# A hybrid attention and convolution block: narrow tap rows, even halves of the latents, early last sums and other costs in the list scheduler

## The chip, the cores and the metric

The kernel runs on one core of a Trainium2 chip. Five engines work at once and are kept in step by semaphores: PE (TensorE, matmuls), DVE (VectorE), ACT (ScalarE), POOL (GpSimd) and SP (SyncE, which issues the DMAs here). The metric is the device time of one execution in microseconds, lower is better. It is a median of several runs; the trace comes from one further execution, the profiled one.

## The reference, cut to what matters

One layer of a residual block on 512 tokens of width 1024, all in float32:

```
mod = silu(c) @ W_ada + b_ada        # shift, scale, gate of the mixer, shift, scale, gate of the MLP
h   = rms_norm(x) * (1 + scale1) + shift1
z   = h @ w_in                       # [GLU 2048 | q latent 384 | kv latent 256 | rotary key 64 | gates 2048]
A:  u = ua * sigmoid(ub); u = causal depthwise conv(u, 31 taps); y_a = silu(layer_norm(u)) @ w_conv_out
B:  q, k, v from rms_norm of the latents; causal attention of 8 heads; y_b = o @ w_attn_out
x  += gate1 * rms_norm((sigmoid(g_a) * y_a + sigmoid(g_b) * y_b) @ w_out)
h   = rms_norm(x) * (1 + scale2) + shift2
x  += gate2 * rms_norm(relu(h @ w_mlp_in)^2 @ w_mlp_out)
```

The six parts of `mod`, 1024 numbers each, are needed before anything that uses them: the first two ahead of all of `z`.

## The kernel before, in words

**Three matmuls for one.** Every float32 operand is split into a rounded high part and a low remainder (`split` and class `W`: a CAST on ACT writes the high part, a TENSOR_TENSOR on DVE the low one). A product is high by high, high by low and low by high (`mm3`, three matmuls). So each weight tile costs a DMA, an ACT cast, a DVE subtraction, and then matmuls of 128 rows by up to 512 columns.

**The order.** Nothing is issued while the program is written. `Planner.record` notes each operation with a cost (`Planner.cost`), and `Planner.plan` is a list scheduler: it simulates the engines and one DMA pipe with those costs and lets each engine take, of the operations that are ready, the one with the earliest due time (`dead`, counted back from the PE order) less a bonus (`hurry`). PE takes its operations in program order, apart from a few that are put ahead. From the simulated times the two SBUF arenas (`f_arena` for raw floats, `r_arena` for split parts) and PSUM get their places, and the plan is made again with the buffers that result, `PASSES` times. In the end each engine runs a fixed list, strictly in that order; an instruction that waits holds up all that stands behind it on its engine.

**The stages**, in order:

- The first products. `ada_load` brings the columns of W_ada for a group of 128-column slices k of shift1 and scale1; DVE sums them over the partitions' eight row blocks (`KGRP`, SCALAR_TENSOR_TENSOR with `cT`), PE adds over partitions (four matmuls by `ones`), DVE writes `mod`. Then `first_products(k)` makes h of slice k (two ACT ACTIVATEs with `mod`, one DVE subtraction) and multiplies it with the first seven GLU column blocks (`g1_load`, 128x896 of w_in per k; 21 matmuls per k). The last slices are k = 6 and k = 7.
- The small loads. The bias and gain vectors, the positions and the convolution's taps `conv_w` (31 rows of 1024 floats, one DMA of 31x1024) are loaded on the side. After the first products PE transposes them to columns; the taps take eight transposes of 31x128 each and a DVE copy into `cw`.
- The latents (`lat_gemm`). The 704 columns of q latent, kv latent and rotary key are made as 512 columns (weights in four units of 2x512) and 192 columns (two units of 4x192), 96 matmuls each. `lat_norm` normalizes them: per token tile two Squares with a sum on ACT, two ACT Identities of 128x1 and two POOL powers of 128x1 (`rstd`), two ACT multiplications.
- The rest of the GLU, and the convolution: 248 DVE operations of 128x512 (`conv_ops`), which `pump` and the planner spread over the stages as filler: 31 taps for each of eight channel tiles, 240 of them SCALAR_TENSOR_TENSOR with `cw`.
- Attention of eight heads (`proj`, `scores`, `pv`); DVE applies the mask to four score tiles of each head. Then y_b, the gates, the LayerNorm of the convolution (transposes, a statistic on ACT and DVE, a power, diagonal matrices that PE multiplies by `ones`), y_a, and, on DVE along the way, the rest of W_ada (`ada_units`, 128x1024 SCALAR_TENSOR_TENSOR with `cT`).
- `w_out`, the norm behind it, then the MLP. Its second product goes over the hidden units in chunks with a Strassen-like scheme (`strassen`, `banked`): sums of products are added on DVE into `f_arena`, and in the last chunk each finished 128x512 block gets its square sum on ACT, a power on POOL, and two DVE operations before it is stored.

## Time and profile before

| | us |
|---|---|
| median of 3 runs (833.59 to 836.13) | 834.04 |
| the profiled execution, its own time | 832.68 |
| its span, first to last instruction | 830.9 |
| busy in it: PE | 805.1 (97%) |
| busy: DVE | 686.6 (83%) |
| busy: ACT | 422.4 (51%) |
| busy: POOL | 26.4 (3%) |

The granted TensorE clock was 0.994 over the span. The profile lists almost all instructions under one line (L388 before), since a helper issues them; rows are told apart by operation, tiles and shape. In a timeline row stand the start, the time from start to end of a group of like instructions, engine, operation, tiles, shapes and count, and in square brackets the engine's idle time before it and who ended it. Some matmul records are missing from the trace, so that a count can be a little low.

### The profile page before, as it was taken

What the parts mean: (1) busy time and instruction counts of PE and PEld (TensorE: products, weight loads), DVE (VectorE), ACT (ScalarE), POOL (GpSimd) and SP (SyncE); (2) the same over time, 40 slices, a digit from 0 to 9 for tenths busy, and PEclk for the clock granted to TensorE, in tenths of its full rate; (3) what the DMA queues carried; (4) which work ended last, traced back from release to release, by engine and by line L of the source; (5) the groups of instructions that cost most, each with busy time, mean ns of one, the idle gap of its engine ahead of it and who ended that gap; (6) DMA issues with size and microseconds to landing.
All of it is one profiled execution on the core that took longest, in us unless ns stands there. A gap on an engine that the chain in (4) does not pass through costs nothing.

```text
span 830.9 us, 10647 instructions
## 1 busy us (share of the span) xinstructions
PE 805.1 (97%) x3940; PEld 672.5 (81%) x3940; DVE 686.6 (83%) x1012; ACT 422.4 (51%) x712; POOL 26.4 (3%) x84
## 2 busy tenths in 40 slices
PE   6989999999999999999999989999999999999995
PEld 3867888889987888888877879888888888888884
DVE  4979989999999999998999589298529993975696
ACT  5364273275884356218424387375346354554642
POOL 2001020000000000000000020000000000000001
PEclk9999999999999999999999999999999999999998
DMA  9998423201464140062799362065014831660302
GB/s 309 321 301 261 153 70 95 71 27 44 135 176 116 40 126 26 26 229 76 277 341 374 118 205 79 27 195 160 0 51 149 277 131 52 193 212 1 102 0 103
DMA packets 86824, 117.28 MB, mean 141 GB/s; under 512 B 7275, under 2 KB 60628, under 8 KB 86771
## 3 DMA queue, kind: packets, MB, share of 16 engines
q1 hardware_dynamic: 86770, 116.59, 43.6%
q8 instruction: 31, 0.51, 0.2%
q14 instruction: 23, 0.18, 0.1%
HBM read 108.18 MB, written 8.39 MB: 140 GB/s over the span
## 4 chain that ended last, share of the span: by engine, by line
PE 87%; DVE 6%; DMA 4%; ACT 2%; issue 1%; POOL 0%; POOLq 0%; DVEq 0%; ACTq 0%; SPq 0%
PE psum L388 87%; DVE f_arena L388 4%; DMA f_arena<-in_w_in_dram 2%; DVE r_arena L388 1%; ACT f_arena L388 1%; DMA f_arena<-in_w_out_dram 1%; ACT r_arena L388 1%; POOL stats L388 0%; DMA f_arena<-in_x_dram 0%; DMA f_arena<-in_w_ada_dram 0%; ACT stats L388 0%; POOLq L1630 0%; DVE mod L388 0%; DVEq L1630 0%; DVE cols L388 0%
## 5 line engine op out<-in xcount | busy, mean ns | idle before, releaser
L388 PE MATMUL psum<-r_arena 128*128 128x512 f32 (+3 forms) x3592 | 765.7, 373 | 8.5 <-ACT r_arena L388 3.6
L388 PEld LDWEIGHTS psum<-r_arena 128*128 128x128 f32 x3592 | 631.3, 189 | 126.8 <-ACT r_arena L388 4.9
L388 DVE TENSOR_TENSOR r_arena<-f_arena,r_arena 128x1024 fp32r<-128x1024 f32 (+4 forms) x232 | 248.1, 1093 | 97.2 <-PE psum L388 56.2
L388 ACT CAST r_arena<-f_arena 128x1024 fp32r<-128x1024 f32 (+4 forms) x222 | 209.3, 967 | 189.7 <-PE psum L388 123.5
L388 DVE SCALAR_TENSOR_TENSOR f_arena<-f_arena,cw 128x512 f32<-128x512 f32 x240 | 164.5, 748 | 0.0
L388 ACT ACTIVATE f_arena<-psum 128x512 f32<-128x512 f32 x64 | 38.1, 598 | 131.4 <-PE psum L388 124.6
L388 DVE TENSOR_TENSOR f_arena<-f_arena 128x1024 f32<-128x1024 f32 (+3 forms) x78 | 77.3, 1006 | 5.5 <-ACT f_arena L388 3.6
L388 ACT ACTIVATE f_arena<-f_arena 128x512 f32<-128x512 f32 (+3 forms) x100 | 58.5, 606 | 13.5 <-DVE f_arena L388 12.6
L388 DVE SCALAR_TENSOR_TENSOR f_arena<-f_arena,cT 128x256 f32<-128x256 f32 (+2 forms) x84 | 55.3, 705 | 0.2
L388 PE MATMUL psum<-ident,f_arena 128*128 128x128 f32 (+1 forms) x240 | 34.4, 283 | 7.5 <-DVE f_arena L388 7.5
L388 PEld LDWEIGHTS psum<-ident,f_arena 128*128 128x128 f32 (+1 forms) x240 | 28.9, 146 | 12.8 <-DVE f_arena L388 8.2
L388 DVE TENSOR_TENSOR f_arena<-psum,f_arena 128x512 f32<-128x512 f32 x52 | 35.4, 687 | 4.4 <-PE psum L388 4.3
L388 ACT CAST r_arena<-psum 128x512 fp32r<-128x512 f32 (+2 forms) x57 | 30.3, 567 | 16.6 <-PE psum L388 16.4
L388 DVE TENSOR_TENSOR r_arena<-psum,r_arena 128x512 fp32r<-128x512 f32 (+2 forms) x57 | 35.7, 658 | 2.5 <-ACT r_arena L388 1.9
L388 POOL TENSOR_TENSOR stats<-stats,nhalf 128x1 f32<-128x1 f32 x24 | 16.8, 708 | 485.4 <-ACT stats L388 485.4
L388 ACT COPY f_arena<-psum 128x512 f32<-128x512 f32 (+4 forms) x42 | 19.9, 501 | 22.1 <-PE psum L388 21.9
L388 ACT ACTIVATE r_arena<-f_arena 128x512 fp32r<-128x512 f32 (+3 forms) x20 | 13.0, 648 | 18.7 <-DVE f_arena L388 16.2
L388 DVE CUSTOM_DVE_ANT_0 f_arena<-psum,mask 128x128 f32<-128x128 f32 (+3 forms) x32 | 15.2, 487 | 2.6 <-PE psum L388 2.5
L388 DVE SCALAR_TENSOR_TENSOR f_arena<-f_arena 128x512 f32<-128x512 f32 (+1 forms) x18 | 13.4, 747 | 0.3
L388 DVE SCALAR_TENSOR_TENSOR f_arena<-f_arena,psum 128x512 f32<-128x512 f32 x16 | 11.0, 685 | 3.1 <-PE psum L388 2.6
L388 DVE TENSOR_SCALAR f_arena<-f_arena,stats 128x1024 f32<-128x1024 f32 x8 | 6.0, 752 | 8.4 <-POOL stats L388 8.4
L388 DVE SCALAR_TENSOR_TENSOR f_arena<-psum,stats,f_arena 128x512 f32<-128x512 f32 x8 | 5.6, 748 | 8.5 <-POOL stats L388 8.3
(94 smaller groups left out, 188.0 us busy)
## 6 DMA issues: line engine op xcount, KB each, us to landing
f_arena<-in_w_ada_dram SPq DMA_DIRECT2D x16, 1024.0 KB, 8.2
f_arena<-in_w_mlp_in_dram SPq DMA_DIRECT2D x32, 512.0 KB, 4.3
f_arena<-in_w_mlp_out_dram SPq DMA_DIRECT2D x32, 512.0 KB, 5.2
f_arena<-in_w_in_dram SPq DMA_DIRECT2D x28, 512.0 KB, 4.7
f_arena<-in_x_dram SPq DMA_DIRECT2D x8, 512.0 KB, 8.0
f_arena<-in_w_ada_dram SPq DMA_DIRECT2D x16, 256.0 KB, 5.7
f_arena<-in_w_ada_dram SPq DMA_DIRECT2D x8, 512.0 KB, 6.4
h_spill<-r_arena SPq DMA_DIRECT2D x16, 256.0 KB, 4.1
```

Source lines behind the costliest of these rows:

```text
L388: getattr(self.real[o.eng], o.fn)(*o.a, **o.k)
```

## The change

- The taps are loaded as rows of 128 floats (512 B), 248 of them, in three DMAs of 128, 112 and 8 rows, and transposed in two matmuls (128 and 120 columns) instead of eight.
- `lat_gemm` makes two halves of 352 columns (eight weight units of 2x352) instead of 512 and 192.
- `lat_norm` folds the mean's factor into the Squares and takes one Identity of 128x8 and one power of 128x8 for all eight norms; all multiplications come behind it. While that power is planned, POOL's result counts as 4000 ns late (`SLOW`).
- The sums of the MLP's last chunk get the bonus `HG` (`banked`).
- The planner's costs are others: a DMA issue 375 for 475 ns, a DMA's time by its packets (13 ns and 0.0385 ns per byte of a row, over 16 engines) instead of its bytes, its tail 1100 for 910 ns, twice its own time ahead of its due time; a matmul at least 109 ns and 13.3 ns over its columns, where 64 and 2.5 stood; 213 ns for a float32 matmul of one column. `PASSES` is 14 for 8. Since costs set due times, the order of all engines and the places in the arenas are others.

```
-PASSES = 8
+PASSES = 14
+SLOW = 4000.0
...
         if fn == "dma_start":
-            return 475.0, 2000.0
+            return 375.0, 2000.0
...
             if ins[0].dtype == F32:
-                return max(53.5, n / 2.4 + 2) * 4, 190.0
-            return max(64.0, n / 2.4 + 2.5), 190.0
+                return (213.0 if n == 1 else max(53.5, n / 2.4 + 2) * 4), 190.0
+            return max(109.0, n / 2.4 + 13.3), 190.0
...
+        o.post += self.slack if eng == "pool" else 0.0
...
-            o.dma = b
+            n = min(self.run(outs[0]), self.run(ins[0]), 4096)
+            o.dma = b * (13.0 + 0.0385 * n) / (16 * n)
...
-            lat = o.post + (o.dma / 180.0 if o.dma else 0.0)
+            lat = o.post + (2.0 * o.dma if o.dma else 0.0)
...
-                        dma_free = st + o.dma / 360.0
-                        o.t1 = dma_free + 910.0
+                        dma_free = st + o.dma
+                        o.t1 = dma_free + 1100.0
...
-        cwr = fa.alloc(D)
-        sp.dma_start(out=fa.v(cwr)[:TAPS, :], in_=conv_w)
+
+        cwr = fa.alloc(2 * P)
+        cw_rows = conv_w.rearrange("t (a p) -> (t a) p", p=P)
+        for r0, r1, at in ((0, P, 0), (P, P + 112, 0), (P + 112, TAPS * KD, 112)):
+            c0 = P if r0 else 0
+            sp.dma_start(out=fa.v(cwr)[at:at + r1 - r0, c0:c0 + P], in_=cw_rows[r0:r1])
...
-        for ct in range(KD):
-            pe.transpose(pb.v(bc)[:, 128 + ct * 32:128 + ct * 32 + TAPS], fa.v(cwr)[:TAPS, ct * P:(ct + 1) * P],
-                         ident[:TAPS, :TAPS])
+        for i, n in enumerate((P, TAPS * KD - P)):
+            pe.transpose(pb.v(bc)[:, (1 + i) * P:(1 + i) * P + n], fa.v(cwr)[:n, i * P:(i + 1) * P], ident[:n, :n])
...
         def lat_gemm():
+            NL = (QL + KL + DR) // 2
...
-                w = wunit(w_in, k0, C_QL, 2, 512)
+                w = wunit(w_in, k0, C_QL, 2, NL)
...
-            ws = [wunit(w_in, kh, C_R2, 4, 192) for kh in (0, 4)]
+            ws = [wunit(w_in, kh, C_QL + NL, 2, NL) for kh in range(0, KD, 2)]
...
         def lat_norm():
+            s = stat(4 * NT)
             for t in range(NT):
-                s = stat(4)
...
-                rstd(s[:, 2:3], s[:, 0:1], 1.0 / QL)
-                rstd(s[:, 3:4], s[:, 1:2], 1.0 / KL)
...
+            plan.slack = SLOW
+            rstd(s[:, 2 * NT:], s[:, :2 * NT], 1.0)
+            plan.slack = 0.0
...
             def banked(mi, nh, bs):
+                plan.hurry = HG if ch == NCH - 1 else 0.0
+                add_block(mi, nh, bs)
+                plan.hurry = 0.0
```

What this does to the lists is seen at three places. The first is ACT at the end of the first products. ACTIVATEs with `mod` make h of slices k = 4, 5, 6 and 7 in pairs (one to `r_arena`, one to `f_arena`); CASTs of 128x896 are weights of the first products, of 128x512 those of the later GLU tiles, of 128x1024, 768 and 704 those of the latents. Before:

```order
27 L388 ACTIVATE r_arena<-f_arena,mod 128x512
28 L388 ACTIVATE f_arena<-f_arena,mod 128x512
29 L388 CAST r_arena<-f_arena 128x896
30 L388 CAST r_arena<-f_arena 128x512
31 L388 ACTIVATE r_arena<-f_arena,mod 128x512
32 L388 ACTIVATE f_arena<-f_arena,mod 128x512
33 L388 CAST r_arena<-f_arena 128x512
34 L388 CAST r_arena<-f_arena 128x1024 x3
35 L388 CAST r_arena<-f_arena 128x768
36 L388 CAST r_arena<-f_arena 128x1024
37 L388 ACTIVATE r_arena<-f_arena,mod 128x512
38 L388 ACTIVATE f_arena<-f_arena,mod 128x512
```

and now:

```order
28 L405 ACTIVATE r_arena<-f_arena,mod 128x512
29 L405 ACTIVATE f_arena<-f_arena,mod 128x512
30 L405 CAST r_arena<-f_arena 128x896
31 L405 ACTIVATE r_arena<-f_arena,mod 128x512
32 L405 ACTIVATE f_arena<-f_arena,mod 128x512
33 L405 CAST r_arena<-f_arena 128x896
34 L405 CAST r_arena<-f_arena 128x512
35 L405 CAST r_arena<-f_arena 128x704 x2
36 L405 ACTIVATE r_arena<-f_arena,mod 128x512
37 L405 ACTIVATE f_arena<-f_arena,mod 128x512
```

The cast of a GLU tile no longer stands ahead of the pair of k = 6, and ahead of the pair of k = 7 stand two casts for the latents in place of five.

The second is DVE at the sixth head. ISA rows with `mask` are its four masked score tiles (the ISA rows of 128x1 read their sums), and SCALAR_TENSOR_TENSOR with `cw` is the convolution's filler. Before:

```order
249 L388 SCALAR_TENSOR_TENSOR f_arena<-f_arena,cw 128x512 x3
250 L388 ISA f_arena<-psum,mask 128x128
251 L388 ISA f_arena 128x1
252 L388 ISA f_arena<-psum,mask 128x256
253 L388 ISA f_arena 128x1
254 L388 SCALAR_TENSOR_TENSOR f_arena<-f_arena,cw 128x512
255 L388 ISA f_arena<-psum,mask 128x384
256 L388 ISA f_arena 128x1
257 L388 RECIPROCAL f_arena<-f_arena 128x1 x2
258 L388 SCALAR_TENSOR_TENSOR f_arena<-f_arena,cw 128x512
259 L388 ISA f_arena<-psum,mask 128x512
```

and now:

```order
264 L405 SCALAR_TENSOR_TENSOR f_arena<-f_arena,cw 128x512 x3
265 L405 ISA f_arena<-psum,mask 128x128
266 L405 ISA f_arena 128x1
267 L405 SCALAR_TENSOR_TENSOR f_arena<-f_arena,cw 128x512
268 L405 ISA f_arena<-psum,mask 128x256
269 L405 ISA f_arena 128x1
270 L405 RECIPROCAL f_arena<-f_arena 128x1
271 L405 SCALAR_TENSOR_TENSOR f_arena<-f_arena,cw 128x512
272 L405 ISA f_arena<-psum,mask 128x384
273 L405 ISA f_arena 128x1
274 L405 RECIPROCAL f_arena<-f_arena 128x1
275 L405 SCALAR_TENSOR_TENSOR f_arena<-f_arena,cw 128x512
```

One more filler operation stands among the tiles, and more stand ahead of them: over the whole list, of the 240 filler operations 109 stood ahead of the sixth head's last mask tile before and 124 do now, and 113 ahead of the eighth's, where it is 130 now.

The third is DVE at the start of `w_out`. SCALAR_TENSOR_TENSOR with `psum` are the last of the sixteen that the GLU tiles and `co_evac` make, which `w_out`'s products need; the operations of 128x1024 with `cT` (28 of them SCALAR_TENSOR_TENSOR, 4 TENSOR_SCALAR) are the late sums of W_ada; TENSOR_TENSOR of 128x1024 are low parts of weights. Before:

```order
418 L388 SCALAR_TENSOR_TENSOR f_arena<-f_arena,cT 128x1024
419 L388 SCALAR_TENSOR_TENSOR f_arena<-f_arena,psum 128x512
420 L388 TENSOR_TENSOR r_arena<-f_arena,r_arena 128x512
421 L388 TENSOR_TENSOR f_arena<-f_arena 128x512
422 L388 SCALAR_TENSOR_TENSOR f_arena<-f_arena,psum 128x512
423 L388 TENSOR_SCALAR f_arena<-f_arena,cT 128x1024
424 L388 TENSOR_TENSOR f_arena<-f_arena 128x512
425 L388 SCALAR_TENSOR_TENSOR f_arena<-f_arena,cT 128x1024
426 L388 TENSOR_TENSOR r_arena<-f_arena,r_arena 128x1024
427 L388 SCALAR_TENSOR_TENSOR f_arena<-f_arena,cT 128x1024
428 L388 TENSOR_TENSOR r_arena<-f_arena,r_arena 128x1024
429 L388 SCALAR_TENSOR_TENSOR f_arena<-f_arena,cT 128x1024 x3
```

and now:

```order
436 L405 SCALAR_TENSOR_TENSOR f_arena<-f_arena,psum 128x512
437 L405 TENSOR_TENSOR r_arena<-f_arena,r_arena 128x512
438 L405 TENSOR_TENSOR f_arena<-f_arena 128x512
439 L405 TENSOR_TENSOR r_arena<-f_arena,r_arena 128x1024
440 L405 TENSOR_TENSOR r_arena<-f_arena,r_arena 128x512
441 L405 SCALAR_TENSOR_TENSOR f_arena<-f_arena,cT 128x1024
442 L405 TENSOR_TENSOR r_arena<-f_arena,r_arena 128x1024 x4
443 L405 SCALAR_TENSOR_TENSOR f_arena<-f_arena,psum 128x512 x2
444 L405 TENSOR_TENSOR f_arena<-f_arena 128x512 x2
445 L405 TENSOR_TENSOR r_arena<-f_arena,r_arena 128x1024
446 L405 TENSOR_TENSOR r_arena<-f_arena,r_arena 128x512 x2
447 L405 TENSOR_TENSOR r_arena<-f_arena,r_arena 128x1024 x2
```

Behind the last of the sixteen stood 17 of the 32 late sums before, and 8 do now (those of the MLP's gate, far behind): nine of them have moved ahead of it.

On PE, 31 matmuls stand now between the last transposes of the LayerNorm and its matmuls by `ones`, where 44 stood; and the gate row's four matmuls by `onesr`, which had 24 others between them, now follow each other.

37 lines of the change are left out of this document (26 added, 11 removed).

## The prediction

> **What bounds the kernel now.** I read the chain of waits first, then the busy times by stage (the windows), then the timeline of the stages that stand out. From the chain (start, length, what, count):
>
> ```profile
> 50.23 10.22 DMA f_arena<-in_w_in_dram
> 69.76 178.40 PE psum L388 x1041
> 248.81 163.60 PE psum L388 x745
> 431.07 6.41 DMA f_arena<-in_w_out_dram
> 490.70 328.19 PE psum L388 x1544
> ```
>
> From 69.76 on the chain is PE, broken only around 412 to 447 and 475 to 490. Ahead of 69.76 it goes through DMAs and DVE. The windows (busy time and count of PE, PEld, DVE, ACT, POOL, then the granted clock, the DMA share and GB/s) say how much PE loses where:
>
> ```profile
> 0.00:70.00 70.00, 59.34 (x272) 43.56 (x272) 50.55 (x120) 37.68 (x56) 6.89 (x56) 1.00 0.98 305
> 70.00:250.00 180.00, 179.65 (x1046) 158.43 (x1047) 168.63 (x331) 101.66 (x229) 8.65 (x16) 1.00 0.35 108
> 70.00:434.42 364.42, 364.07 (x1886) 310.54 (x1887) 344.86 (x588) 183.13 (x368) 10.06 (x17) 1.00 0.39 123
> 430.00:450.00 20.00, 17.22 (x71) 13.18 (x70) 16.87 (x19) 8.21 (x10) 0.00 (x0) 0.91 1.04 380
> 475.00:500.00 25.00, 22.32 (x141) 19.33 (x140) 20.87 (x29) 21.22 (x44) 6.31 (x7) 1.00 0.59 204
> ```
>
> PE idles 10.7 us in the first 70, 0.35 in the next 364, 2.8 at 430 to 450 (at a clock of 0.91, so that it loses more there) and 2.7 at 475 to 500. DVE is the second limit: of the 364.42 us it is busy 344.86 and idle only 19.6, 11.4 of them before 250. What can be won is PE work itself, the start, and those two gaps; what can be lost is that DVE comes too late.
>
> **The start.** Timeline rows (idle before and its releaser in brackets):
>
> ```profile
> 41.95 0.24 SPq L388 DMA_DIRECT2D f_arena<-in_conv_w_dram  x1
> 46.96 0.16 DVE L388 TENSOR_TENSOR mod<-psum,cols 128x1 f32<-128x1 f32 x1
> 52.51 0.50 PE L388 MATMUL psum<-ones,f_arena 128*128 128x1 f32 x4
> 52.87 2.35 PE L388 MATMUL psum<-r_arena 128*128 128x512 f32 x9
> 53.08 0.62 ACT L388 CAST r_arena<-f_arena 128x512 fp32r<-128x512 f32 x1 [6.12 <-DMA f_arena<-in_w_in_dram]
> 55.91 0.50 PE L388 MATMUL psum<-r_arena 128*128 128x512 f32 x1 [0.69 <-DVE r_arena L388]
> 56.77 0.15 DVE L388 TENSOR_TENSOR mod<-psum,cols 128x1 f32<-128x1 f32 x1
> 56.91 4.60 PE L388 MATMUL psum<-r_arena 128*128 128x512 f32 x19 [0.50 <-DVE r_arena L388]
> 61.42 0.81 ACT L388 ACTIVATE r_arena<-f_arena,mod 128x512 fp32r<-128x512 f32 x1
> 62.28 0.50 PE L388 MATMUL psum<-r_arena 128*128 128x512 f32 x1 [0.78 <-ACT r_arena L388]
> 63.72 4.87 PE L388 MATMUL psum<-r_arena 128*128 128x512 f32 x20 [0.93 <-DVE r_arena L388]
> ```
>
> `mod` of k = 6 is there at 47, but its ACTIVATEs stand on ACT behind the cast of a GLU tile, which waits 6.12 us for a DMA, to 53.08. `mod` of k = 7 could follow the sums of 52.51, and comes at 56.77, since DVE stands on the late ACTIVATEs of k = 6; its own ACTIVATEs run at 61.42, behind five casts of latent weights. PE gets its last first products at 63.72 and ends them at 68.59. The DMA that held ACT was issued next to `conv_w`; what was issued before and after it (KB, us to landing), and the DMA engines between 44.5 and 50:
>
> ```profile
> f_arena<-in_w_ada_dram SPq DMA_DIRECT2D x3, 256.0 KB, 5.9
> f_arena<-in_w_in_dram SPq DMA_DIRECT2D x2, 256.0 KB, 10.2
> DMA  9999999999999976554232010107696786859999
> ```
>
> Before `conv_w` a transfer lands in 5.9 us, behind it in 10.2, and meanwhile the share of the 16 engines falls to zero: one engine still works on something, 4.3 us long. (The Trainium skill, DMA: Bandwidth & Descriptors, section on why a DMA increments its semaphore by 16, says that a transfer is split over the largest number up to 16 that divides its outermost sizes; that makes one engine of 31 rows, 16 of 128 and of 112 rows, eight of 8. The share of zero agrees.)
>
> After the change 112, 128 and 8 rows lie on many engines, and the lists help apart from that: the casts that waited stand behind the ACTIVATEs of k = 6, and two casts instead of five ahead of those of k = 7. Against it, about 0.87 MB (GLU weights of 256 and 512 KB, and the taps) now stand ahead of the last W_ada loads in SP's queue: at the 305 GB/s of the first row 2.9 us, less the 4.3. So the inputs come no later. If PE runs from 52.87 without a wait, the 50 matmuls recorded there (9, 1, 19, 1 and 20) take 50 x 0.227 = 11.4 us (21.76 us for 96, below) and end at 64.2: **-4.4 us**, from -1.5 (inputs 2.9 us later after all) to -5.2 (of the 10.7 us that PE idles in the first 70, the brackets here hold 2.9; a tenth of the other 7.8 on top).
>
> **PE's own work.** The two parts of the latents, a stretch of 256-column matmuls, and the old tap transposes:
>
> ```profile
> 75.62:97.38 21.76, 21.76 (x98) 18.02 (x96) 20.89 (x33) 7.24 (x10) 0.00 (x0) 1.00 0.65 210
> 97.38:108.08 10.70, 10.70 (x98) 10.70 (x96) 10.69 (x17) 4.66 (x17) 0.00 (x0) 1.00 0.13 38
> 492.24 7.68 PE L388 MATMUL psum<-r_arena 128*128 128x256 f32 x62
> 70.80 0.67 PE L388 MATMUL psum<-ident,f_arena 31*128 31x31 f32 x8
> ```
>
> A matmul of 512 columns takes 227 ns, one of 192 takes 111, one of 256 takes 124. The 192s are dear: PE's weight load is busy all of their 10.70 us. For 352 columns the line from 256 to 512 gives 124 + 96 x 0.402 = 163 ns, columns alone 156, the line from 192 to 512 169. So 192 x 0.163 = 31.3 against 32.46 us; I take the middle of 0 and 2.5: **-1.3**. (The Trainium skill, TensorE: Matmul & The Clock Gate, Part 1, "Wait — 56ns, not 53.3ns?", gives N / 2.4 GHz + about 2.5 ns start to start. By it 96 x (215.8 + 82.5) and 192 x 149.2 are the same 28.6 us, and the halves save nothing. The trace speaks against it for narrow matmuls: 111 ns where it has 82.5.)
>
> Eight transposes become two: **-0.3** of 0.67, either way by 0.2. The single power costs nothing:
>
> ```profile
> L388 POOL TENSOR_TENSOR stats<-stats,nhalf 128x1 f32<-128x1 f32 x24 | 16.8, 708 | 485.4 <-ACT stats L388 485.4
> L388 POOL TENSOR_TENSOR lns<-lns,nhalf 128x4 f32<-128x4 f32 x1 | 1.4, 1402 | 256.2 <-DVE lns L388 256.2
> 129.88 2.78 PE L388 MATMUL psum<-ident,f_arena 128*128 128x128 f32 x24
> ```
>
> Width 8 lies between 0.7 and 2 x 1.4 us, and PE has other work from 108.08 to the latents' transposes at 129.88. Without that cover it would cost up to 2.8.
>
> **DVE's order.** Filler and late sums (start, length, count):
>
> ```profile
> 344.91 8.05 DVE L388 SCALAR_TENSOR_TENSOR f_arena<-f_arena,cw 128x512 f32<-128x512 f32 x12
> 440.95 3.67 DVE L388 SCALAR_TENSOR_TENSOR f_arena<-f_arena,cT 128x1024 f32<-128x1024 f32 x3
> 434.42 0.69 DVE L388 SCALAR_TENSOR_TENSOR f_arena<-f_arena,psum 128x512 f32<-128x512 f32 x1 [0.83 <-PE psum L388]
> 437.29 1.20 PE L388 MATMUL psum<-r_arena 128*128 128x512 f32 x4 [2.44 <-ACT r_arena L388]
> ```
>
> The 17 fillers that now stand ahead of the last head are 17 x 0.67 = 11.4 us, just what DVE idled before 250. The nine late sums that moved ahead of the last `co_evac` are 8 x 1.22 + 0.75 = 10.5 us more DVE work ahead of 434.42. PE will want that operation 6.0 us earlier than before (4.4 + 1.3 + 0.3). DVE without any idle would reach it at 434.42 - 19.6 + 10.5 - 4.4 = 420.9, PE wants it at 428.4: DVE may idle 7.5 us on the way, where it idled 19.6. With the fillers in the holes 19.6 - 11.4 = 8.2 are left: PE waits **+0.7**, between 0 and 12.1 if no hole is filled.
>
> For it, the sums no longer hold the buffer that the `w_out` load of 431.07 waited for, and PE's wait of 2.44 (then 0.27) at 437 goes: **-2.7**, from 0 to -4.8 (of the 71 matmuls at 430 to 450, 63 at 227 ns and eight transposes at the 111 ns of narrow ones fill 15.2 of the 20 us).
>
> The LayerNorm's cover shrinks from 44 matmuls to 31:
>
> ```profile
> 365.48 0.38 PE L388 MATMUL psum<-ident,f_arena 128*128 128x128 f32 x2
> 373.04 0.67 DVE L388 TENSOR_SCALAR f_arena<-ident,lns 128x128 f32<-128x128 f32 x3
> 375.69 1.75 PE L388 MATMUL psum<-f_arena,ones 128*128 128x128 f32 x14
> ```
>
> From the last transposes to the diagonals DVE needed 7.85 us (365.86 to 373.71); 31 x 0.227 = 7.0 cover it: **+0.8**, from 0 to 2.8 if DVE comes late.
>
> **The end and the norm.** The last add:
>
> ```profile
> 815.76 5.83 PE L388 MATMUL psum<-r_arena 128*128 128x512 f32 x25
> 823.37 0.69 DVE L388 TENSOR_TENSOR f_arena<-psum,f_arena 128x512 f32<-128x512 f32 x1
> ```
>
> PE is done at 821.59; the last add runs at 823.37, behind the scaling of the block before. It stands behind that scaling in the new list too: **-0.2**, from 0 to -1.8. The norm behind `w_out` (the gap at 475) has another order on ACT and POOL, of which I can't tell the sign: 0, give or take 2.4.
>
> **The sum.** -4.4 - 1.3 - 0.3 + 0.7 - 2.7 + 0.8 - 0.2 = -7.4 us. On the profiled execution (832.68, span 830.9) that is 825.3 and a span of 823.5; the median of 834.04 lies 1.4 above that execution, so the time to compare with it is 834.04 - 7.4 = 826.6.
>
> **The rivals.** About 0.3%, 2.5 us, is what a measurement of this kernel can tell from no change.
>
> 1. DVE comes too late at `w_out`. If the holes in DVE's list are waits for ACT's weights and for PSUM that filler can't fill, all 19.6 us stay, PE waits 12.1 and the whole is -7.4 - 0.7 + 12.1 = +4.0: 838.0, slower. For it: DVE already idles only 5% of that stretch, and carries 10.5 us more into it. Against it: the fillers amount to just what it idled. It is slower from 18.1 us of idle time on; between 13 and 18 the gain is eaten up: some 833.5, no change to tell.
> 2. The start doesn't move: the 10.2 us were the queue's and not the taps', and 0.87 MB more stand in it. Without the -4.4 DVE has time enough (no +0.7): 834.04 - 3.7 = 830.3; if the gap at `w_out` stays by half, 831.7. For it: GB/s stand at 305 over the first 70 us, a full queue. Against it: the share of zero.
> 3. The halves save nothing, as the page's rule has it. In rows: if the weight load, not the columns, set the 163 ns, 169 would stand: 192 x 0.169 = 32.4, and 827.9. The weight load is not busy all of the time at 512 (18.02 of 21.76), which speaks against it.
>
> **How the numbers follow.** My forecast gets 0.56, rival 1 in full 0.14 and by half 0.13, rival 2 0.12 (half of it beyond 0.3%), rival 3 0.05. Faster is 0.56 + 0.06 + 0.05 = 0.67, same 0.13 + 0.06 = 0.19, slower 0.14. The range goes from all gains in full (-5.2 - 2.5 - 0.3 - 4.8 - 1.8 = -14.6, 819.4) to 834.5, just above no change, which leaves out rival 1 in full and little else.
>
> **What would show it.** Right: ACT's wait at the GLU cast under 2 us and PE's first products done by 64.5; landings near 6 us behind the taps; the latents in about 31.3 us; no PE wait for `w_out`; DVE idle 6 to 10 us from there to the last `co_evac`. Wrong: PE waits on DVE between 100 and 430 of more than 3 us in sum, a chain that runs through DVE there, or first products that end after 67.

## The result and the profile after

The changed kernel takes 827.85 us, a median of 5 runs (826.63 to 829.63). The kernel before, run beside it, takes 833.59 us (5 runs, 831.19 to 836.13). The ratio is 0.9934, 95% interval 0.9908 to 0.996, so the kernel is faster by 0.7%.

The profiled execution of after took 829.63 us with a span of 827.8, which is 1.78 above the median of its kernel; that of before, 832.68, is 0.91 below its own. So the two traces differ by only 3.05 us where the medians differ by 5.74. What follows compares the traces and so explains the 3.05.

First the windows of after (start and end, length, busy time and count of PE, PEld, DVE, ACT and POOL, granted clock, DMA share, GB/s):

```profile
0.00:70.00 70.00, 58.66 (x257) 43.79 (x258) 50.24 (x119) 34.25 (x53) 6.61 (x55) 0.95 0.97 303
70.00:434.42 364.42, 362.82 (x1878) 310.12 (x1877) 355.48 (x600) 188.85 (x369) 7.70 (x10) 1.00 0.42 137
430.00:450.00 20.00, 20.00 (x90) 16.57 (x89) 16.36 (x19) 8.82 (x10) 0.00 (x0) 1.00 0.90 304
475.00:500.00 25.00, 24.25 (x161) 21.20 (x160) 20.64 (x29) 20.09 (x41) 4.92 (x6) 1.00 0.54 185
```

The last two rows had 17.22 and 22.32 us of PE before: the gap at `w_out` is closed (20.00 of 20.00 at full clock) and the one at the norm is down from 2.7 to 0.75 us. The first row is worse than before: PE idles 11.3 us where it idled 10.7, and the granted clock over the stretch is 0.95 where it was 1.00. In the chain of waits of after, the start shows the same (start, length, what, count):

```profile
31.89 7.13 DMA f_arena<-in_w_ada_dram
42.11 2.46 DVE f_arena L405 x8
44.81 3.42 DVE f_arena L405 x11
48.52 0.82 ACT r_arena L405
49.39 105.24 PE psum L405 x524
...
251.71 115.89 PE psum L405 x526
367.60 0.74 issue
368.34 99.93 PE psum L405 x455
...
504.08 306.85 PE psum L405 x1388
```

From 154.66 to 186.11 the chain runs through DVE in pieces (with 7.89 us of PE among them), and again in short pieces at 211 to 215 and 244 to 251, which it did not before; the idle time that is counted there is small, 0.57 us for DVE in all between 100 and 430. From 368 it is PE alone up to 468.

The timeline of the start, PE and DVE and ACT in after:

```profile
44.73 0.94 ACT L405 CAST r_arena<-f_arena 128x896 fp32r<-128x896 f32 x1 [7.37 <-DMA f_arena<-in_w_in_dram]
47.52 0.64 PE L405 MATMUL psum<-ones,f_arena 128*128 128x1 f32 x4 [1.66 <-DVE f_arena L405]
48.20 0.16 DVE L405 TENSOR_TENSOR mod<-psum,cols 128x2 f32<-128x2 f32 x1
49.39 2.07 PE L405 MATMUL psum<-r_arena 128*128 128x512 f32 x4 [1.23 <-ACT r_arena L405]
51.97 8.66 PE L405 MATMUL psum<-r_arena 128*128 128x512 f32 x31
61.06 11.17 PE L405 MATMUL psum<-r_arena 128*128 128x512 f32 x48
```

`mod` of k = 4, 5 comes at 48.20, where it came at 42.87 before. PE waits 1.66 us for the sums that it is made from, and then 1.23 for ACT, which makes h with it. At the same time the granted clock is halved for two windows of 3.41 us each, until 54.8; the 31 matmuls take 0.28 us each instead of 0.23. The window of that stretch:

```profile
48.00:54.80 6.80, 5.58 (x17) 4.52 (x17) 6.80 (x22) 5.45 (x8) 0.12 (x1) 0.50 1.03 316
```

Part of the cause is far ahead of it, in SP's queue. SP in after:

```profile
23.59 0.33 SPq L405 DMA_DIRECT2D f_arena<-in_conv_w_dram  x1
25.08 0.29 SPq L405 DMA_DIRECT2D rows<-in_g_pre_mlp_dram  x1
...
30.38 0.35 SPq L405 DMA_DIRECT2D f_arena<-in_conv_w_dram  x1
30.84 0.40 SPq L405 DMA_DIRECT2D f_arena<-in_w_ada_dram  x1
```

Nine small loads (two of the three tap pieces, six vectors and the positions) stand in a row from 23.59 to 30.38, ahead of the first W_ada piece of slices 4 and 5, which leaves at 30.84 now. Before, it left at 24.58:

```profile
24.58 0.40 SPq L388 DMA_DIRECT2D f_arena<-in_w_ada_dram  x1
```

The share of the DMA engines shows the difference. SP's window 28 to 30 (length, granted clock, DMA share, GB/s) of before:

```profile
28.00:30.00 2.00, 1.00 1.06 362
```

And the same window of after:

```profile
28.00:30.00 2.00, 1.00 0.09 24
```

The DMA engines ran dry. In the trace the issues take eight semaphores in turn, and each waits for the landing of the one eight places before it; so with eight small loads in a row nothing large is on its way. Nothing in the prediction looked at this stretch: it reasoned about the queue from 42 on.

That is not all of the 5.3 us. `mod` of k = 2, 3 is late already, before and after:

```profile
29.80 0.16 DVE L388 TENSOR_TENSOR mod<-psum,cols 128x2 f32<-128x2 f32 x1
33.59 0.16 DVE L405 TENSOR_TENSOR mod<-psum,cols 128x2 f32<-128x2 f32 x1 [0.23 <-PE psum L405]
```

Its W_ada pieces left at 14.18 and 14.49, ahead of the small loads in both kernels. `mod` of k = 1 comes at 23.19 before and at 24.20 in after. So of the 5.3 us 1.0 is lost up to there, 2.8 from there to `mod` of k = 2, 3, whose sums DVE does later (from 20.14 to 28.29 before, from 22.79 to 32.36 in after), and 1.5 from there to `mod` of k = 4, 5, where the engines run dry.

The latents, and the new power, as groups of instructions (count, then busy time in all and mean of one in ns; the mean of a matmul holds its latency):

```profile
L405 PE MATMUL psum<-r_arena 128*128 128x352 f32 x192 | 30.8, 322 | 0.0
L405 POOL TENSOR_TENSOR stats<-stats,nhalf 128x8 f32<-128x8 f32 x1 | 3.1, 3059 | 31.1 <-ACT stats L405 31.1
```

30.8 us against 32.46, or 160 ns a matmul.

**The account of the 3.05 us.** PE's idle time and its time at half clock, stage by stage, from these rows and those of before. The 24 transposes of the latents begin at 130.96 (129.88 before) although 2.0 us less of PE work lies ahead of them (1.65 of the latents, 0.3 of the taps): the start lost 1.1 + 2.0 = 3.1. Most of it is the half clock: 5.58 us of busy PE at 0.50 are worth 2.8, as an estimate, and the idle time grew by 0.7. From 70 to 434.42 PE idles 1.6 instead of 0.35: 1.25 lost, 0.74 of it at the LayerNorm. From 430 to 520 it idles 0.83 instead of 5.45 (both from that window's PE time, 89.17 and 84.55 of 90), and one window of 3.41 us at half clock at 438.7 is gone, worth 1.7: 6.3 won. PE work 2.0 won. From the last matmul to the span's end it is 8.8 instead of 9.3: 0.5 won. That makes -4.4, and 1.4 us of loss are left over.

Most of them lie in the stretch where the chain runs through DVE, from the latents' transposes to PE's first matmul on raw floats of `f_arena` (248.81 before, 251.71 in after). The windows, before and after:

```profile
129.88:248.81 118.93, 118.58 (x727) 106.58 (x725) 112.41 (x246) 74.91 (x166) 0.00 (x0) 1.00 0.30 91
130.96:251.71 120.75, 119.88 (x729) 105.98 (x727) 119.75 (x257) 75.11 (x168) 0.00 (x0) 1.00 0.29 88
```

For the same matmuls the stretch is 1.8 us longer, of which only 0.5 is counted as idle: the recorded ends of matmuls are modelled, and short waits vanish in PE's busy time. Two matmuls there start 0.60 and 0.75 us behind the one before them, in place of 0.23, each when a DVE operation of the chain ends (185.46 + 0.61 and 214.44 + 0.70).

### The profile page after: what moved, and what is told of

Its sections match the earlier page's. It is cut to its first block, busy times and chain, and to the rows that moved or that the text cites. A ratio compares the mean times of both kernels' runs of the same rounds, so it can differ in the third digit from the quotient of the medians.

```text
span 827.8 us, 10653 instructions
## 1 busy us (share of the span) xinstructions
PE 805.3 (97%) x3934; PEld 674.6 (81%) x3934; DVE 684.3 (83%) x1014; ACT 421.6 (51%) x707; POOL 23.1 (3%) x77
## 4 chain that ended last, share of the span: by engine, by line
PE 84%; DVE 6%; DMA 4%; ACT 3%; issue 1%; SPq 1%; POOL 1%; POOLq 0%; DVEq 0%
PE psum L405 84%; DVE f_arena L405 4%; ACT f_arena L405 2%; DMA f_arena<-in_w_ada_dram 2%; DVE r_arena L405 1%; ACT r_arena L405 1%; DMA f_arena<-in_w_in_dram 1%; SPq L405 1%; DMA f_arena<-in_x_dram 1%; POOL stats L405 1%; ACT stats L405 0%; POOLq L1659 0%; DVEq L1659 0%; DVE mod L405 0%; DVEq L405 0%
## 5 line engine op out<-in xcount | busy, mean ns | idle before, releaser
L405 ACT ACTIVATE f_arena<-f_arena 128x512 f32<-128x512 f32 (+4 forms) x100 | 58.6, 603 | 21.3 <-DVE f_arena L405 20.2
L405 DVE TENSOR_TENSOR f_arena<-psum,f_arena 128x512 f32<-128x512 f32 x52 | 35.0, 681 | 11.3 <-PE psum L405 11.3
L405 PE MATMUL psum<-ident,f_arena 128*128 128x128 f32 x234 | 35.3, 291 | 7.7 <-DVE f_arena L405 7.6
L405 PEld LDWEIGHTS psum<-ident,f_arena 128*128 128x128 f32 x234 | 28.5, 149 | 14.3 <-DVE f_arena L405 9.7
L405 ACT CAST r_arena<-psum 128x512 fp32r<-128x512 f32 (+2 forms) x57 | 30.1, 563 | 11.6 <-PE psum L405 11.0
L405 ACT COPY f_arena<-psum 128x512 f32<-128x512 f32 (+5 forms) x42 | 19.9, 500 | 25.3 <-PE psum L405 25.2
L405 POOL TENSOR_TENSOR stats<-stats,nhalf 128x1 f32<-128x1 f32 (+1 forms) x17 | 14.0, 825 | 483.8 <-ACT stats L405 483.7
L405 ACT ACTIVATE f_arena<-f_arena,lnh 128x512 f32<-128x512 f32 x16 | 12.4, 810 | 3.8 <-DVE f_arena L405 3.7
L405 DVE SCALAR_TENSOR_TENSOR f_arena<-f_arena,psum 128x512 f32<-128x512 f32 x16 | 10.7, 681 | 1.8 <-ACT f_arena L405 1.8
```

Source lines behind the costliest of these rows:

```text
L405: getattr(self.real[o.eng], o.fn)(*o.a, **o.k)
```

## The experiments

Each ratio is against the kernel before, run beside it on the same chip (832.68 us median in the first four runs, 831.45 in the second four, 831.26 in the last four).

**The taps alone.** The kernel before, with the 31 rows of taps as two DMAs:

```
-        sp.dma_start(out=fa.v(cwr)[:TAPS, :], in_=conv_w)
+        sp.dma_start(out=fa.v(cwr)[:16, :], in_=conv_w[:16])
+        sp.dma_start(out=fa.v(cwr)[16:TAPS, :], in_=conv_w[16:])
```

> The kernel before with one edit: the 31 rows of taps in two DMAs of 16 and of 15 rows, the second in the old place. Theory R (31 rows lie on one DMA engine, and all behind them wait 4.3 us for that one): ACT's wait of 6.12 us at the GLU cast falls below 2, landings behind the taps from 10.2 to about 6 us, and PE gets its last first products 2 to 4.4 us sooner; time 829 to 832. Rival Q (the queue, not the one engine, makes the wait): the wait stays above 5 us, time 833 to 834.5.

Measured: 829.66 us (12 runs, 827.54 to 831.48), ratio 0.997 [0.9956, 0.9984]. The DMA issues from 42 to 44.5 in this kernel (KB each, median us to landing):

```profile
f_arena<-in_w_in_dram SPq DMA_DIRECT2D x2, 256.0 KB, 3.9
f_arena<-in_conv_w_dram SPq DMA_DIRECT2D x1, 60.0 KB, 4.2
```

And its timeline of PE behind the last `ones` of the first products:

```profile
53.97 11.64 PE L388 MATMUL psum<-r_arena 128*128 128x512 f32 x50
65.54 0.25 PE L388 MATMUL psum<-ident,rows 37*128 37x37 f32 x1
```

10.2 us became 3.9, ACT's cast no longer waits, and the 50 matmuls run without a break in 11.64 us, where the prediction gave them 11.4. The latents' transposes come 3.15 us earlier. So the first half of the prediction's start step holds: the 31 rows in one DMA were the cause, and splitting them is worth 3 us at the start. Further on this order gains at `w_out` and loses at the norm, where PE waits 3.97 us at 486.35 (2.43 before) with two windows of half clock. (The Trainium skill, DMA: Bandwidth & Descriptors, section on why a DMA increments its semaphore by 16, has the rule by which 31 rows get one engine and 16 rows sixteen, and 15 rows fifteen; this trace agrees, 10.2 against 3.9 us for what landed behind them.)

**The new costs alone.** The kernel before with the planner's costs and the 14 passes of the change, and nothing else of it (costs and passes were not tried apart). Its core:

```
-PASSES = 8
+PASSES = 14
...
-            return max(64.0, n / 2.4 + 2.5), 190.0
+            return max(109.0, n / 2.4 + 13.3), 190.0
...
-            o.dma = b
+            n = min(self.run(outs[0]), self.run(ins[0]), 4096)
+            o.dma = b * (13.0 + 0.0385 * n) / (16 * n)
```

> The kernel before with only the planner's new costs and PASSES 14; taps, latents, norms and last sums as before. Theory P (the gaps at 437 and 490 went because of the new order): PE doesn't wait at w_out, worth 5 to 6, and nothing else moves by more than 3: time 826 to 831. Rival (they went because the halves and the narrow taps left other places in the arena): PE still waits 2 us or more at w_out, time 832.5 to 836.

Measured: 842.72 us (841.48 to 843.79), ratio 1.013 [1.0111, 1.015]. Slower by 10, outside of what both expectations had. The start loses 4.4 us at the latents' transposes, with two windows of half clock there and a third at 140.8; PE waits 3.13 us at 140.18 and 2.18 at 172.40 for DVE; the gap at `w_out` is gone here too (PE busy 89.16 of the 90 us from 430). POOL's timeline in the middle of this kernel, first one power and then two of them as one group:

```profile
119.46 4.55 POOL L405 TENSOR_TENSOR stats<-stats,nhalf 128x1 f32<-128x1 f32 x1 [42.75 <-ACT stats L405]
119.46 8.24 POOL L405 TENSOR_TENSOR stats<-stats,nhalf 128x1 f32<-128x1 f32 x2 [42.75 <-ACT stats L405]
```

And DVE's at the same time:

```profile
116.80 6.71 DVE L405 SCALAR_TENSOR_TENSOR f_arena<-f_arena,cw 128x512 f32<-128x512 f32 x10
123.43 0.54 DVE L405 TENSOR_SCALAR f_arena<-f_arena,cw,cols 128x512 f32<-128x512 f32 x1
123.89 3.39 DVE L405 SCALAR_TENSOR_TENSOR f_arena<-f_arena,cw 128x512 f32<-128x512 f32 x5
135.06 1.83 DVE L405 TENSOR_TENSOR r_arena<-f_arena,r_arena 128x768 fp32r<-128x768 f32 x2 [7.77 <-ACT r_arena L405]
```

The first power of 128x1 takes 4.55 us and the second ends 8.24 us after the first began; the least that one takes is 0.54. Both end just behind a break in DVE's run of two-input filler: the first at 124.01, 0.04 us after the one TENSOR_SCALAR in it, the second at 127.70, 0.42 after the run's end at 127.28. DVE then idles 7.77 us behind ACT, which has waited 3.20 and 2.48 us for these two powers.

**The small loads held back.** The changed kernel, with ten small loads (six vectors, the positions and the three tap pieces) issued behind the sums of slices 4 and 5:

```
+            if ks == LATE:
+                plan.after = len(plan.ops) - 1
+                plan.hurry = 0.0
+                for o_, i_ in small:
+                    sp.dma_start(out=o_, in_=i_)
+                plan.after = None
```

> The changed kernel with its ten small loads (six vectors, the positions, three tap pieces) held back until the sums of slices 4 and 5 are done, so that SP issues the loads of W_ada and w_in for the first products one behind the other. Theory S (SP keeps at most eight DMAs out, and nine small loads in a row let the DMA pipe run dry from 27.3 to 31.4, so that W_ada of slices 4 and 5 comes late, PE idles and its granted clock falls to 0.50): the DMA share stays above 0.8 from 20 to 40, the clock at 1.00 throughout, and PE reaches the 24 transposes of the latents 3 to 7 us sooner than at 130.96; time 821 to 825. Rival B (these loads wait for their place in f_arena, not for SP): the gap stays, PE's point stays within 1 us, time 827 to 829.

Measured: 827.33 us (824.34 to 828.18), ratio 0.994 [0.9921, 0.9959], the same as the change. The DMA share stays above 1.0 from 20 to 50 us, the first W_ada piece of slices 4, 5 leaves at 23.29, but `mod` of k = 4, 5 still comes at 47.96, one window of half clock is left (at 50.4), and the transposes come only 1.3 us earlier. So neither expectation holds as a whole: theory S has the share right and the rest wrong; rival B has the time right, but its gap is gone. DVE's first sum of these slices, in the timeline of after:

```profile
39.12 0.35 DVE L405 TENSOR_SCALAR f_arena<-f_arena,cT 128x256 f32<-128x256 f32 x1 [0.94 <-DMA f_arena<-in_w_ada_dram]
```

In this kernel:

```profile
38.82 0.35 DVE L406 TENSOR_SCALAR f_arena<-f_arena,cT 128x256 f32<-128x256 f32 x1
```

In after that sum waits for its DMA; with the small loads held back it waits for nothing but its place in DVE's list, at nearly the same time. So the empty DMA engines are one cause, and the order of DVE in the new list is another. The times of `mod` show the size of each (us; the kernel with the old DMA model comes further down):

| kernel | `mod` of k = 1 | of k = 2, 3 | of k = 4, 5 | first stretch | second stretch |
|---|---|---|---|---|---|
| before | 23.19 | 29.80 | 42.87 | 6.6 | 13.1 |
| after | 24.20 | 33.59 | 48.20 | 9.4 | 14.6 |
| small loads held back | 25.55 | 34.92 | 47.96 | 9.4 | 13.0 |
| old DMA model | 25.34 | 31.99 | 45.41 | 6.7 | 13.4 |

Holding the loads back wins the second stretch back, some 1.5 us, and nothing of the first, where 2.8 are lost; the old DMA model wins back the first as well. Why `mod` of k = 1 comes 1.3 us later here than in after, which hides what was won, isn't shown, and no run changes DVE's order alone.

**The old taps back in.** The changed kernel, with the taps as one DMA of 31x1024 and eight transposes.

```
-        cwr = fa.alloc(2 * P)
-        cw_rows = conv_w.rearrange("t (a p) -> (t a) p", p=P)
...
+        cwr = fa.alloc(D)
+        sp.dma_start(out=fa.v(cwr)[:TAPS, :], in_=conv_w)
```

> The changed kernel with the taps as before: one DMA of 31 rows, eight transposes. Theory S has two small loads fewer in the row ahead of W_ada, but R has the one slow engine back: between -2 and +4.4 against 827.9, that is 826 to 832.3; PE's start then shows which is the larger. Rival (the narrow rows are what wins): PE reaches the latents' transposes 4 us later than at 130.96, time 832 or more.

Measured: 830.99 us (829.84 to 832.19), ratio 0.9984 [0.9973, 0.9995]. The transposes come 2.25 us later than in after. The narrow taps are worth some 3 us inside the change as they are outside of it.

**All but the costs.** The changed kernel with the planner's costs and passes of before.

```
-PASSES = 14
+PASSES = 8
...
-            return 375.0, 2000.0
+            return 475.0, 2000.0
...
-            return max(109.0, n / 2.4 + 13.3), 190.0
+            return max(64.0, n / 2.4 + 2.5), 190.0
...
-            o.dma = b * (13.0 + 0.0385 * n) / (16 * n)
+            o.dma = b
```

> All parts of the change but the recorded durations: the list schedule has the durations and the eight passes of the kernel before, with the narrow taps, the halves, the one power and the hurried last sums. In the list PE's first products stand ahead of the sums of k = 2, 3 as before (20 and 4, not 31 and 6). Theory A (the new durations lose the time in the start, by the order of PE and DVE there, and it is the same durations that close the gap at w_out): the 24 latent transposes come at about 124.6 us (126.73 with split taps alone, less 2.1 of PE work) and no window of half clock lies before 70; the gap at w_out may come back, and the time is 820 if it does not and 827 if it does. Theory B (the parts crowd SP's queue at the start whatever the durations): latent transposes at 129 to 131, time 828 or more.

Measured: 825.58 us (824.98 to 826.07), ratio 0.9928 [0.9916, 0.9941]. Theory A holds in the main: transposes at 125.83 (it had 124.6), 9.5 us of idle PE in the first 70, no half clock anywhere before the end. At `w_out` PE waits once, 1.18 us, and from 430 to 520 it idles 2.85, so that the gap is back in part and the time lies between the theory's two.

**The halves alone**, in the kernel before.

```
+            NL = (QL + KL + DR) // 2
...
-                w = wunit(w_in, k0, C_QL, 2, 512)
+                w = wunit(w_in, k0, C_QL, 2, NL)
...
-            ws = [wunit(w_in, kh, C_R2, 4, 192) for kh in (0, 4)]
+            ws = [wunit(w_in, kh, C_QL + NL, 2, NL) for kh in range(0, KD, 2)]
```

> The kernel before with the latents in two halves of 352 columns and nothing else. My term: PE's own work falls by 1.65 us (192 matmuls of 160 ns against 227 and 111), the latent transposes come 1 to 2 us earlier than 129.88, and the time falls by 1 to 2 us to about 831, unless DVE or the gap at w_out takes it back. Rival (a start-to-start cost that only counts columns): no change of PE's work, 833.

Measured: 825.68 us, ratio 0.9925 [0.9909, 0.994] (the median of six runs; one shows 2872.84, which nothing here explains, the other five lie between 823.74 and 826.39, with a median of 825.01). 5.8 us won or a little more, where I expected 1 to 2. The matmuls give what was expected (192 x 160 ns again, 30.8 us; transposes at 127.49, 2.4 earlier). The rest is the gap at `w_out`, which closes by the order alone: PE idles 1.5 us from 430 to 520 instead of 5.45. In this list 11 us more of PE's work stands between those transposes and the matmuls by `onesr` (127.49 to 443.10, instead of 129.88 to 434.22). That this is why the gap closes is not shown: with halves and split taps, below, it stays closed with these matmuls at 435.75.

**The old norms back in.** The changed kernel with eight powers of 128x1 in place of one of 128x8. With them go `SLOW` and the place of the multiplications: each token tile's stand behind its own powers again.

```
-            rstd(s[:, 2 * NT:], s[:, :2 * NT], 1.0)
...
+                rstd(s[:, 2:3], s[:, 0:1], 1.0 / QL)
+                rstd(s[:, 3:4], s[:, 1:2], 1.0 / KL)
```

> The changed kernel with the latents' norms as before: eight powers of 128x1 on POOL instead of one of 128x8. My prediction's term: nothing, 827.9 give or take 1. Rival, from the run with the durations alone, where PE waited 3.13 us at 140 and 2.18 at 172 for DVE, which stood behind ACT, which stood behind POOL's powers to 132.8: PE waits 2 to 5 us between 130 and 180 and the time is 830 to 833.

Measured: 834.39 us (832.94 to 835.67), ratio 1.0036 [1.0023, 1.0049]. The rival wins, by a little more than it asked: 6.5 us above the change by the medians (8 by the ratios), and the change as a whole would have been slower. The row of each engine that makes the chain (DVE's filler, POOL, ACT, DVE, PE), in this kernel:

```profile
99.50 10.02 DVE L405 SCALAR_TENSOR_TENSOR f_arena<-f_arena,cw 128x512 f32<-128x512 f32 x15
104.93 5.00 POOL L405 TENSOR_TENSOR stats<-stats,nhalf 128x1 f32<-128x1 f32 x1 [2.28 <-ACT stats L405]
109.96 1.03 ACT L405 ACTIVATE f_arena<-f_arena,stats 128x384 f32<-128x384 f32 x2 [4.92 <-POOL stats L405]
112.89 1.23 DVE L405 TENSOR_TENSOR r_arena<-f_arena,r_arena 128x1024 fp32r<-128x1024 f32 x1 [3.37 <-ACT r_arena L405]
166.68 0.69 PE L405 MATMUL psum<-ident,f_arena 128*128 128x128 f32 x2 [3.26 <-DVE f_arena L405]
```

One power takes 5.00 us, until 109.93, 0.41 after DVE's run ends at 109.52; ACT waits for it with weights of the next products behind; DVE loses 3.37 us, and has no idle time from 115.8 on with which to make them good; PE pays 3.26 us 54 us later, with a window of half clock on top at 166.3. That is some 5 us (3.26, and 1.7 for a window of 3.41 us at half clock). The latents' transposes come 1.3 us later than in after (132.26), which is lost in the first 74 us, ahead of the first of these powers at 101.09.

**Without the hurry of the last sums**, in the changed kernel (`banked`).

```
-                plan.hurry = HG if ch == NCH - 1 else 0.0
+                plan.hurry = 0.0
```

> The changed kernel without the hurry for the last adds of the last chunk (the rest of the list may shift a little with it). My prediction's term for that edit was 0.2 us: time 828 give or take 0.5, and from the last matmul to the span's end 9.3 us as before the change, where the changed kernel has 8.7. Rival (the last add stood behind the scaling by the old list alone): 1.8 us slower, 829.7.

Measured: 828.91 us (828.02 to 829.18), ratio 0.9969 [0.9957, 0.998]. From the last matmul to the span's end it is 8.8 us with and without the edit (827.1 - 818.34 and 827.85 - 819.08), and the last add stands behind the scaling of the block before in both. So the edit does nothing there, and the 9.3 us that I expected don't come back; the 0.5 us that the end is shorter than before come from elsewhere in the list. The time is 1.1 us above after's by the medians and 3 by the ratios, whose intervals just overlap; the profiled spans (827.1 and 827.85) show nothing of it.

**The DMA model or the matmul costs?** Two halves of the new costs. First the changed kernel with DMAs modelled as before:

```
-            return 375.0, 2000.0
+            return 475.0, 2000.0
...
-            n = min(self.run(outs[0]), self.run(ins[0]), 4096)
-            o.dma = b * (13.0 + 0.0385 * n) / (16 * n)
+            o.dma = b / 360.0
...
-                        o.t1 = dma_free + 1100.0
+                        o.t1 = dma_free + 910.0
```

> The changed kernel, but the list schedule models DMAs as before the change (475 ns of issue, bytes at 360 GB/s, landing 910 ns later); the recorded durations of PE, the slack of POOL and the 14 passes stay. In its list PE's first products stand as before the change (19 and 6 ahead of the sums of k = 2, 3). Theory D (the DMA model alone moves the start): the latent transposes come at 124.6 to 126.5 us, PE idles 9.5 us in the first 70 with no half clock there, and the time is 824 to 827, with no wait of PE at w_out. Theory P (PE's durations move the start or the middle): transposes at 129 to 131, time 827 to 830.

Measured: 823.49 us (822.72 to 824.35), ratio 0.99 [0.9885, 0.9915]. The window of its start:

```profile
0.00:70.00 70.00, 61.20 (x280) 45.59 (x281) 52.26 (x125) 36.53 (x56) 8.24 (x62) 1.00 1.02 320
```

And PE's timeline there, the only wait above 0.7 us behind 10 us and the last first products:

```profile
46.65 2.38 PE L404 MATMUL psum<-r_arena 128*128 128x512 f32 x9 [0.94 <-ACT r_arena L404]
54.28 12.76 PE L404 MATMUL psum<-r_arena 128*128 128x512 f32 x55
```

Transposes at 125.76, 5.2 us earlier than in after, a clock of 1.00 in that row, 8.8 us of idle PE, and no gap at `w_out` (89.17 of the 90 us from 430). Then the mirror image:

```
-                return (213.0 if n == 1 else max(53.5, n / 2.4 + 2) * 4), 190.0
-            return max(109.0, n / 2.4 + 13.3), 190.0
+                return max(53.5, n / 2.4 + 2) * 4, 190.0
+            return max(64.0, n / 2.4 + 2.5), 190.0
```

> The mirror image: the changed kernel with the PE durations that the list schedule had before, and the new DMA model. In its list PE's first products stand as after the change (32 and 7 ahead of the sums of k = 2, 3). Theory D: transposes at 129 to 132 us, a window or two of half clock at 48 to 55, PE idles 11 us in the first 70, time 828 to 831. Theory P: transposes at 124.6 to 126.5, time under 826.

Measured: 827.55 us (825.85 to 828.54), ratio 0.995 [0.9936, 0.9963]. Idle PE of 11.1 us in the first 70 and a window of half clock at 49.4, as theory D has it; transposes at 128.44 and the time lie between the two theories, nearer to D. The DMA model is worth 4.4 us by the medians, which come from different batches, and 2.8 by the ratios (0.99 against 0.9934). PE's durations are worth nothing that the time shows with the new DMA model (827.55 against 827.85). With the old one they, or the 14 passes that go with them, win some 2 us (823.49 against 825.58, ratios 0.99 and 0.9928).

**Halves and split taps**, two edits in the kernel before, both shown above: `NL` columns in `lat_gemm`, and

```
+        sp.dma_start(out=fa.v(cwr)[:16, :], in_=conv_w[:16])
+        sp.dma_start(out=fa.v(cwr)[16:TAPS, :], in_=conv_w[16:])
```

> The kernel before with two edits: the latents in halves (alone 825.68) and the taps as two DMAs of 16 and 15 rows (alone 3.1 us earlier at the latent transposes). If the two are independent, the transposes come at 124.5 to 125.5 us, PE idles 8.3 us in the first 70, and the time is 822 to 824 as long as the gap at w_out stays closed as with the halves alone. If that gap was closed by a chance of the order, and opens again, 826 to 828.

Measured: 823.71 us (822.21 to 824.89), ratio 0.9904 [0.9889, 0.992]. Transposes at 125.84, 8.2 us of idle PE in the first 70. The gap at `w_out` stays closed, and a wait of 2.43 us at the norm, at 481.6, is left. These two edits do at least as much as the whole change.

**The old latents back in.** The changed kernel with 512 and 192 columns.

```
-                w = wunit(w_in, k0, C_QL, 2, NL)
+                w = wunit(w_in, k0, C_QL, 2, 512)
...
-            ws = [wunit(w_in, kh, C_QL + NL, 2, NL) for kh in range(0, KD, 2)]
+            ws = [wunit(w_in, kh, C_R2, 4, 192) for kh in (0, 4)]
```

> The changed kernel with the latents in 512 and 192 columns again. By PE's work alone 1.65 us more: 829.5. If the halves are worth more than their work (alone in the kernel before they won 5.8, of which 1.65 is PE's work and most of the rest the gap at w_out), the gap at w_out is back, PE waits 2 us or more between 430 and 480, and the time is 831 to 834.

Measured: 829.85 us (827.77 to 831.97), ratio 0.998 [0.9966, 0.9994]. By the medians 2.0 us are lost, about PE's work (1.65); by the ratios, 0.998 against 0.9934, it is 3.8. The trace has the transposes 2.0 us later (132.96), and PE idles 0.8 us from 430 to 520, as in after. So the new costs keep the gap closed without the halves.

Four of these versions take less time than both kernels: 823.49 (the change with the old DMA model), 823.71 (halves and split taps), 825.58 (all but the costs) and 825.68 (the halves alone). All but that one run of 2872.84 lie below the lowest of after, 826.63. They ran in other batches, though: by the ratios the first two (0.99 and 0.9904) lie ahead of after (0.9934) with intervals that just overlap its own, and the other two can't be told from it. The first two can't be told from each other.

## Why the prediction was right, and where it was not

The time was predicted at 826.6 and is 827.85. That it came so near is luck. Between the two traces 3.05 us were won, not the 7.4 of the sum: the start missed by 7.5 us, `w_out` and the norm together gave 3.6 more than was counted, and the rest is that the profiled execution of after lies 1.78 above its median and that of before 1.4 below the one that I added from. Step by step:

1. **What bounds the kernel: right.** PE's own work, the start and the two gaps are where time was won and lost in every run.
2. **The start, -4.4: wrong.** The traces have +3.1. The step failed where it says "So the inputs come no later." The reasoning on the taps was sound (3 us by themselves, ten to four us of landing, 50 matmuls in 11.6), but it looked at SP's queue only from 42 us on, and took the rest of the start as given. The new DMA model had put DVE's sums of slices 2, 3 later (2.8 us) and nine small loads together at 23.6 to 30.4 (1.5 us); with 1.0 lost earlier `mod` came 5.3 us later, PE waited, and the clock was halved for two windows. Of the signs it named, the GLU cast's wait is gone and what landed behind the taps took 5.1 us; but a cast of the first products' own weights now waits 7.37 us, and the first products end at 72.2, behind the 67 that was to show an error. Rival 2 (the start doesn't move) came nearer, but for another reason: the 10.2 us were the taps'.
3. **The latents, -1.3: right,** -1.65 measured. 160 ns for 352 columns lies below the 163 that I took. Rival 3 is refuted: the rule of the Trainium skill (TensorE: Matmul & The Clock Gate, Part 1, "Wait — 56ns, not 53.3ns?"), N / 2.4 GHz + 2.5 ns, would give no gain, and the 192 matmuls of 149 ns that it has here take 160.
4. **The tap transposes, -0.3: right.** 0.67 us became 0.38.
5. **One power costs nothing: right for the trace of before, wrong as a value of the edit.** It took 3.06 us, just over the bound of 2.8, under cover. But in the new order the eight single powers cost some 5 us (of the 6.5 to 8 of that run, 1.3 lie in the start). The prediction counted the work of POOL and its cover on PE; what it lacked is that a POOL operation can stand still through several DVE operations with two inputs, and that ACT and DVE queue behind it.
6. **DVE's order, +0.7 (0 to 12.1): right at `w_out`, and some 1.8 elsewhere.** PE has no wait at `w_out`, and DVE idles 8.9 us between 70 and 434.42, inside the 6 to 10 given; its busy time there grew by 10.6, where 10.5 were counted. But one sign of an error did come, a chain that runs through DVE between 100 and 430, and the stretch from 131 to 252 in which it does is 1.8 us longer. The other sign, waits for DVE of more than 3 us in sum, did not (0.57 counted). Rival 1 had 14% in full and did not come.
7. **The gap at `w_out`, -2.7 (0 to -4.8): right in sign, too small.** The wait (2.7) and the half clock behind it (1.7) went, 4.4 in all. The reason given was too narrow: it need not be the late sums that move. The gap also closes with the halves alone and with the costs alone. It was a feature of one order, and the other orders here have at most a part of it (1.18 us of wait with all but the costs).
8. **The norm, 0 give or take 2.4: -1.9,** inside. The sign could not be told ahead, and the runs don't explain it: it comes and goes from list to list (3.97 us with split taps alone, 2.43 with halves and split taps, 0.75 in the stretch in after).
9. **The LayerNorm, +0.8: right.** PE waits 0.74 us ahead of the matmuls by `ones`:

```profile
360.27 7.33 PE L405 MATMUL psum<-r_arena 128*128 128x512 f32 x31
368.34 2.18 PE L405 MATMUL psum<-f_arena,ones 128*128 128x128 f32 x16 [0.74 <-issue]
```

10. **The end, -0.2: the size is near (-0.5), but it isn't the bonus,** as the run without it shows.

So the parts of the change rank otherwise than the prediction had them: narrow taps about -3, halves -2 by work, almost any new order about -4 at `w_out` with the norm coming and going, one power about -5 in the new order only, and the DMA model +4.4 by the medians or +2.8 by the ratios. What stays open is which term of the DMA model moves the small loads and DVE's sums (the issue time, the time by rows, or the tail), and what the 14 passes do apart from the costs; neither was tried.

## What to carry to other kernels

A list scheduler's costs are not a neutral part of a change: new ones, with 14 passes for 8, made this kernel 10 us slower by themselves, so try the edits with the old costs and the new costs without the edits before judging either. Where an order changes, read the whole of each queue from the first instruction, not only the place that the edit names. And a small operation on POOL between ACT and DVE can be dangerous while DVE streams two-input work: make it once, not eight times.

## What the hardware showed that I had not expected

**POOL can stand still while DVE runs on two SBUF inputs.** A power of 128x1 takes 0.54 us, and 4.55, some 3.7 and 5.00 us in the three cases above, each ending 0.04 to 0.42 us after a break in DVE's run of SCALAR_TENSOR_TENSOR. Not every power fares so. In the kernel with the old norms two others fall into the same unbroken run of DVE, ahead of the one of 5.00, and take 1.56 us together:

```profile
101.09 1.56 POOL L405 TENSOR_TENSOR stats<-stats,nhalf 128x1 f32<-128x1 f32 x2 [19.53 <-ACT stats L405]
```

What makes the difference isn't shown. (The Trainium skill, SBUF — State Buffer, section "Who interferes with whom", says that a DVE instruction with two SBUF inputs contends with a GpSimd instruction that reads SBUF, and calls the port pair that they share an exclusive lock. The three long powers agree, and show more: the block lasted through five to seven DVE instructions in a row, 0.67 us each, not through one.)

**The clock is halved in pieces of 3.41 us.** Two such pieces lie at PE's waits of 1.66 and 1.23 us in after, and one at the 3.26 us of the old norms. (The Trainium skill, TensorE: Matmul & The Clock Gate, Part 1, "What's actually happening", has windows of 3413 ns and a half clock after one that was idle; the traces agree on the length and the half, but here it followed waits as short as 1.5 us.) When a wait brings it on isn't settled: in before 2.44 us at 437 did, and 2.43 at 490 did not; with halves and split taps the same wait of 2.43 did, and with the halves alone 1.47 us at 482 did.

**Small loads empty the DMA engines.** Nine loads of at most 64 KB, issued 0.3 to 2.1 us apart by a queue that has eight semaphores for its loads, brought the share of the engines from 1.07 to 0.09. With these loads held back the share stayed above 1.0.
